# Four pairs of input tiles by seven quarter products over half of the contraction, in a hybrid decoder layer

## The chip, the cores and the metric

The kernel runs on one core of one Trainium2 chip. The metric is device time in microseconds of one execution. The kernel before takes 724.74 us (median of three runs, 724.72 to 724.83).

## What is computed

One layer with two groups of channels side by side, on 1024 tokens and 1024 model channels, in float32. Cut to what matters here:

```python
h = rmsnorm(x, norm_g) * (1.0 + scale[:, None, :]) + shift[:, None, :]
u = h @ w_in                                  # 1024 x 5120
cv, cg, cs, lx, ls = jnp.split(u, [D_CONV, 2 * D_CONV, 3 * D_CONV, 3 * D_CONV + D_LRU], axis=-1)

v = cv * jax.nn.sigmoid(cg)
v = causal_depthwise_conv(v, dw_w, dw_b)      # 31 taps
v = jax.nn.silu(layernorm(v, cln_g, cln_b))
y_conv = (v @ pw2_w + pw2_b) * jax.nn.silu(cs)

xs = causal_depthwise_conv(lx, sc_w, sc_b)    # 4 taps
r = jax.nn.sigmoid(blockdiag(xs, wr) + br)
i = jax.nn.sigmoid(blockdiag(xs, wi) + bi)
a = jnp.exp(-LRU_C * r * softplus(-lam))
hs = linear_scan(a, sqrt(1 - a**2) * (i * xs))
y_lru = hs * jax.nn.silu(ls)

x = x + (1.0 + gate[:, None, :]) * (concat([y_conv, y_lru]) @ w_out)
out = rmsnorm(x, final_g)
```

## The kernel before, in words

**Tiles.** Channels lie on the 128 partitions, tokens along the free dimension. A tile is 128 channels x 1024 tokens; w_in gives 40 of them, numbered by kind: i0 to i7 are the convolution's values (CV), i8 to i15 its GLU gates (CG), i16 to i23 its SiLU gates (CS), i24 to i31 the recurrence's inputs (LX), i32 to i39 its SiLU gates (LS). A contraction over 1024 channels is eight k tiles.

**Three terms.** Each float32 operand is split into a high part in fp32r and the remainder (h and l in the names: uh and ul, whi and wlo). A product is wh x h, wh x l and wl x h, each as one matmul of 128 x 128 by 512 tokens. A plain input tile is 8 k tiles x 3 terms x 2 halves of tokens = 48 matmuls (`mm_k`). The high part is a cast on ACT. The remainder is a subtraction on DVE or GpSimd (POOL in the profile), or ACT writes minus the high part and a transfer on GpSimd's queue adds the original to it (`remainder`, "DMA" in the tables).

**Stages.** First four input tiles while x is normalised (to 56 us); then the slots of the table ORDER, where i is an input tile and g the two gate products of a head of the recurrence; then the recurrence's half of the output projection, its eight output tiles in four pairs (from 471 us), during which the convolution's mean and layer norm are made; then the pointwise projection pw2 and the other half of the output projection; then the last norm.

**Seven products.** The pairs of the second, third and fourth stage already use the seven products of two by two blocks in Winograd's form: two output tiles and two halves of the tokens give a block of four, and the four quarters cost seven products, with sums of weights (S1 to S4) and of tokens (T1 to T4). In the recurrence's pairs (`lru_pair`) this covers half of the contraction, k tiles 0 to 3 (JS); k tiles 4 to 7 are plain halves. Line 1447 is the matmul of these quarters, line 579 that of plain k tiles.

**The convolution.** Its 31 taps run as 16 products of even taps, 16 of sums of neighbouring taps and 15 of odd ones, each over half of the tokens. For most tiles they are multiply-adds on DVE into PSUM (cacc and caccs, line 443); for the tiles in POOLED, ACT makes each product (cq, co) and a transfer on GpSimd's queue adds it into SBUF (es, oo, line 456). csum is the sum of all conv tiles for the mean.

**The order.** A planner (`Plan.order`) lists all operations with a priority, a cost and their dependences, runs a list schedule over PE, ACT, DVE, GpSimd and SP, and emits the instructions in that order; on the chip each engine takes its own in order and waits on semaphores. A slot's priority is its number n; its weights have n - 2.5 (load) and n - 1.4 (split), its evacuation n + 0.5. PSUM holds three tiles of 1024 (mm) and two of 512 (acc), SBUF 47 buffers of one tile (big). `reserve` keeps buffers free of an operation, `S.hold` and `after` make it wait.

**After a gate.** sigmoid, exp, tanh and sqrt on ACT (each change of table is a load), products and a scan on DVE, and the product with the SiLU gate gives y (in sls). yh and yl are its parts, yhs and yls those of the token sums of y0 to y3, held until slot YSLOT.

## Time and profile before

| what | value |
|---|---|
| median of the runs | 724.74 us |
| the profiled execution's span | 723.3 us |
| PE busy | 715.6 us, 3268 matmuls |
| DVE busy | 619.9 us |
| ACT busy | 480.9 us, 44 table loads |
| GpSimd busy | 166.5 us, 169 instructions |
| moved by DMA | 138.06 MB |
| granted TensorE clock, mean | 0.998 |

The span runs from the first to the last instruction; the median is 1.4 us longer than it. A group of instructions is given by line, engine, operation, names of output and inputs without buffer numbers, shapes, count, then busy time and mean ns of one. The time of a matmul in such a group is from its issue to its modelled end and overlaps with the next; the pace is read from the chain in order of time. PEld is the weight load beside the matmul.

### The profile page before, as it was taken

The page shows a single profiled execution, that of the slowest core. Times are in us where ns is not written, and L with a number is a line of the kernel's source. Part 1 is how long each engine was busy: PE and PEld are TensorE (multiplying, and loading weights), DVE is VectorE, ACT ScalarE, POOL GpSimd, SP SyncE. Part 2 cuts the span into 40 slices and gives each one's busy share as a digit, 9 for nine tenths or more (in the row PEclk, how much of TensorE's full clock was granted, in tenths as well). Part 3 has the DMA queues.
Part 4 walks back from the last instruction along what each step waited for, and adds up shares of the span by engine and source line. Part 5 has one row for each costly group of instructions (what it writes and reads, how often), then busy time and mean ns, then how long its engine had stood idle before and what let it go on. Part 6 is the DMA issues. An engine that isn't in the chain of part 4 may idle for free.

```text
span 723.3 us, 9066 instructions
## 1 busy us (share of the span) xinstructions
PE 715.6 (99%) x3268; PEld 596.7 (83%) x3268; DVE 619.9 (86%) x852; ACT 480.9 (66%) x621; POOL 166.5 (23%) x169
## 2 busy tenths in 40 slices
PE   9999999999999999999999999999999999999996
PEld 8888888888888888888888888888888888888886
DVE  7999999989789898789489994998798966999647
ACT  7650689664788956965967879846697635745332
POOL 0036333444534230133221220001101001100001
PEclk9999999999999999999999999999999999999999
DMA  8946439958999997699898896957846755775006
GB/s 334 407 158 191 69 96 239 285 103 197 203 235 211 247 235 154 198 218 233 174 210 225 238 191 144 255 215 169 210 93 145 198 150 140 231 186 181 30 1 232
DMA packets 46635, 138.06 MB, mean 191 GB/s; under 512 B 5264, under 2 KB 16528, under 8 KB 46480
## 3 DMA queue, kind: packets, MB, share of 16 engines
q0 software_dynamic: 19872, 52.88, 41.0%
q1 hardware_dynamic: 25712, 83.71, 32.7%
q10 hardware_dynamic: 1008, 0.92, 0.4%
q8 instruction: 25, 0.41, 0.2%
q14 instruction: 18, 0.15, 0.1%
HBM read 79.11 MB, written 22.54 MB: 141 GB/s over the span
## 4 chain that ended last, share of the span: by engine, by line
PE 98%; DVE 1%; ACT 0%; DVEq 0%; issue 0%
PE ps L579 54%; PE xout L755 6%; PE xpw L755 6%; PE first L888 5%; PE lx L1447 3%; PE ypw L755 3%; PE gate L1308 3%; PE zout L755 2%; PE zpw L755 2%; PE lx L579 2%; PE y L725 1%; PE lc L579 1%; PE yout L755 1%; PE lw L579 1%; PE ld L579 1%; PE late L888 1%
## 5 line engine op out<-in xcount | busy, mean ns | idle before, releaser
L579 PE MATMUL ps<-uh,wlo 128*128 128x512 f32 x576 | 177.4, 389 | 0.0
L579 PE MATMUL ps<-uh,whi 128*128 128x512 f32 x576 | 177.4, 389 | 0.0
L579 PE MATMUL ps<-ul,whi 128*128 128x512 f32 x576 | 177.3, 389 | 0.0
L579 PEld LDWEIGHTS ps<-uh,wlo 128*128 128x128 f32 x576 | 108.1, 188 | 22.5
L579 PEld LDWEIGHTS ps<-ul,whi 128*128 128x128 f32 x576 | 108.1, 188 | 22.4
L579 PEld LDWEIGHTS ps<-uh,whi 128*128 128x128 f32 x576 | 108.0, 188 | 22.4
L424 ACT CAST whi<-raw 128x1024 fp32r<-128x1024 f32 (+1 forms) x44 | 44.9, 1026 | 46.8 <-issue 27.3
L456 POOL DMA_DIRECT2D es<-cq x45 | 40.1, 898 | 135.4 <-ACT cq L432 85.9
L451 POOL TENSOR_TENSOR wlo<-raw,whi 128x1024 fp32r<-128x1024 f32 x16 | 41.0, 2569 | 87.5 <-ACT whi L424 87.1
L432 ACT ACT_TABLE_LOAD x44 | 56.5, 1283 | 1.5 <-PEq L1875 0.7
L443 DVE SCALAR_TENSOR_TENSOR cacc<-v,V,cacc 128x511 f32<-128x511 f32 (+14 forms) x75 | 55.5, 740 | 0.4
L443 DVE SCALAR_TENSOR_TENSOR caccs<-v,V,caccs 128x511 f32<-128x511 f32 (+6 forms) x70 | 52.0, 743 | 1.9 <-ACT caccs L432 1.0
L443 DVE SCALAR_TENSOR_TENSOR caccs<-c,wsum,caccs 128x511 f32<-128x511 f32 (+6 forms) x70 | 52.0, 743 | 1.0
L456 POOL DMA_DIRECT2D oo<-co x39 | 37.5, 995 | 44.8 <-ACT co L432 18.0
L451 DVE TENSOR_TENSOR wlo<-raw,whi 128x1024 fp32r<-128x1024 f32 (+1 forms) x24 | 28.7, 1195 | 8.3 <-ACT whi L424 8.3
L432 ACT ACTIVATE cq<-v,V 128x511 f32<-128x511 f32 (+14 forms) x45 | 31.8, 708 | 4.5 <-DVE modw L443 4.5
L443 DVE SCALAR_TENSOR_TENSOR xs<-ps,V,xs 128x1023 f32<-128x1023 f32 (+2 forms) x24 | 30.6, 1273 | 0.5 <-ACT xs L432 0.5
L432 ACT ACTIVATE cq<-c,wsum 128x512 f32<-128x512 f32 x42 | 29.7, 713 | 0.0
L443 DVE SCALAR_TENSOR_TENSOR modw<-modw,sc 128x1024 f32<-128x1024 f32 x23 | 29.5, 1286 | 0.0
L432 ACT ACTIVATE finsq<-fin 128x512 f32<-128x512 f32 (+2 forms) x14 | 7.9, 570 | 28.5 <-DVE fin L443 15.3
L432 ACT ACTIVATE co<-v,V 128x510 f32<-128x510 f32 (+12 forms) x39 | 26.7, 707 | 0.0
L424 ACT CAST xsh<-xs 128x1024 fp32r<-128x1024 f32 x8 | 8.4, 1050 | 21.8 <-issue 15.9
(447 smaller groups left out, 1592.0 us busy)
## 6 DMA issues: line engine op xcount, KB each, us to landing
raw<-in_w_in_dram SPq DMA_DIRECT2D x36, 512.0 KB, 5.5
modw<-in_mod_w_dram SPq DMA_DIRECT2D x24, 512.0 KB, 8.1
scsd<-scs SPq DMA_DIRECT2D x8, 512.0 KB, 3.9
raw<-in_w_out_dram SPq DMA_DIRECT2D x8, 512.0 KB, 3.6
accd<-acc POOLq DMA_DIRECT2D x8, 512.0 KB, 5.8
rawpw<-in_pw_dram SPq DMA_DIRECT2D x8, 512.0 KB, 4.8
scsr<-scsd SPq DMA_DIRECT2D x8, 512.0 KB, 4.7
rawout<-in_w_out_dram SPq DMA_DIRECT2D x8, 512.0 KB, 3.7
```

The lines of the kernel that those rows point to most:

```text
L424: act.copy(out(), in_())
L432: act.activation(out=out(), in_=in_(), func=func, **kw)
L443: dve.scalar_tensor_tensor(out=out(), in0=in0(), scalar=scalar, in1=in1(), op0=op0, op1=op1, accum_out=accum)
L451: lambda: e.tensor_tensor(out=out(), in0=a(), in1=b(), op=op), prio, r, w,
L456: return S.op("POOL", ISSUE, lambda: pool.dma_start(out(), a(), accum_op=ALU.add), prio, r, w, lag=RATE * n / T, after=after, flight=flight)
L579: pe.matmul(ps()[:, a - off:b - off], k3(lhs)()[:, at, :], rhs[k]()[:, a:b], start=(k == first and lhs is wh and rhs is xh and (a - off) % ...
L725: pe.matmul(to(), half(*lhs)()[:, j * P:j * P + P], half(*rhs)()[:, c0:c1], start=a == "S1" and j == 0 and t == 0, stop=j == KT // 2 - 1 a ...
L755: pe.matmul(half(ps, 0)(), half(*lhs)()[:, j * P:j * P + P], half(*rhs)(), start=start and at == 0 and i == 0, stop=at == len(order) - 1 a ...
L888: pe.matmul(ps()[:, a - off:b - off], fw_part(lhs, k, i * P, i * P + P)(), rhs()[:, a:b], start=k == 0 and lhs is wh and rhs is xh, stop=k ...
L1308: pe.matmul(ps()[:, c0:c1], lhs()[:, j, :], rhs()[:, c0:c1], start=st == 0, stop=st == 2)
L1447: pe.matmul(half(ps, h)(), lhs()[:, o:o + P], half(*rhs)(), start=begin and at == 0 and t == 0, stop=at == len(order) - 1 and t == len(ter ...
```

## The change

**Pairs of input tiles.** The table ORDER gets four entries with a plus: i36+i28, i30+i37, i29+i38 and i22+i18. Such a pair (`duo`) takes two slots. Over k tiles 0 to 3 the four quarters (two tiles, two halves of tokens) come from seven products; over k tiles 4 to 7 each half is a plain sum. w_in is stored with its k tiles in the order 0, 2, 1, 3, 4 to 7, so that a block of weights is contiguous. Four combinations of weights (wz, 256 columns each) are made on GpSimd and split into wsh and wsl; of the second tile only six k tiles are split. The products share two PSUM tiles, up and dn: A11 goes into dn and is copied to up (ACT), S1 into the other half of dn and is copied to wk, and two sums on DVE carry them on.

**Token sums.** From slot 15 on (`token_sums`), GpSimd adds high and low part of h's k tiles 0 to 3, makes the combinations, and splits them (hhs, hls), for all four pairs.

**The convolution.** POOLED goes from tiles 1, 3 and 5 to 1 and 3; tile 5's products become multiply-adds on DVE.

**Beside these.** The order of the other tiles changes, and g5 and g6 change places; four conv tiles instead of three are written out and read back (SPILL); y0 to y3 are written out and read back before their split (YSP); y3, y6 and y7 have their remainder by transfer (YDMA); which engine makes which weight's remainder changes (EARLY, EARLYD, DENG, LRV), and some reserves.

**The order on PE, first pair.** PE, behind A11 and S1 of the first pair (dn27 and up27 are its PSUM tiles, whi27 the first tile's weights, wsh27 and wsl27 the combined ones, uh1 and ul1 k tile 1 of h, hhs01 a token sum, ps29 the plain tile behind the pair):

```order
L599 MATMUL ps29_2781<-uh0_189,whi29_2758 128x512 x2
L599 MATMUL ps29_2781<-ul0_206,whi29_2758 128x512 x2
L599 MATMUL ps29_2781<-uh0_189,wlo29_2767 128x512 x2
L1678 MATMUL up27_2788<-uh1_230,whi27_2678 128x512
L1678 MATMUL up27_2788<-ul1_243,whi27_2678 128x512
L1678 MATMUL up27_2788<-uh1_230,wlo27_2697 128x512
L1678 MATMUL dn27_2754<-hhs01_1813,wsh27_2733 128x512
L1678 MATMUL dn27_2754<-hls01_1850,wsh27_2733 128x512
L1678 MATMUL dn27_2754<-hhs01_1813,wsl27_2746 128x512
L1678 MATMUL dn27_2754<-hhs11_2184,wsh27_2733 128x512
L1678 MATMUL dn27_2754<-hls11_2205,wsh27_2733 128x512
L1678 MATMUL dn27_2754<-hhs11_2184,wsl27_2746 128x512
```

Six matmuls of the next tile stand between S1 and A12, the reader of the copy, and S2 comes in the middle of A12. Before, these slots were 48 matmuls each into one ps.

**The order on PE, where the recurrence's pairs begin.** Before (lx0 and lp0 are PSUM tiles of the first pair, yh7 and yl7 the parts of y7, whi40 weights):

```order
L1447 MATMUL lx0_3855<-yhs11_3891,lsh0_3694 128x512
L1447 MATMUL lx0_3855<-yhs11_3891,lsl0_3745 128x512
L1447 MATMUL lx0_3855<-yls01_3861,lsh0_3694 128x512
L579 MATMUL lp0_3863<-yh7_3837,whi40_3764 128x512 x2
L579 MATMUL lp0_3863<-yl7_3919,whi40_3764 128x512 x2
L579 MATMUL lp0_3863<-yh7_3837,wlo40_3780 128x512 x2
```

and now:

```order
L599 MATMUL lp0_3887<-yh6_3487,whi40_3748 128x512 x2
L599 MATMUL lp0_3887<-yl6_3720,whi40_3748 128x512 x2
L599 MATMUL lp0_3887<-yh6_3487,wlo40_3763 128x512 x2
L1478 MATMUL lx0_3924<-yh0_3774,whi40_3748 128x512
L1478 MATMUL lx0_3924<-yl0_3784,whi40_3748 128x512
L1478 MATMUL lx0_3924<-yh0_3774,wlo40_3763 128x512
L1478 MATMUL lx0_3924<-yh2_3848,whi40_3748 128x512
L1478 MATMUL lx0_3924<-yl2_3870,whi40_3748 128x512
L1478 MATMUL lx0_3924<-yh2_3848,wlo40_3763 128x512
L599 MATMUL lp0_3887<-yh7_3827,whi40_3748 128x512 x2
L599 MATMUL lp0_3887<-yl7_3862,whi40_3748 128x512 x2
L599 MATMUL lp0_3887<-yh7_3827,wlo40_3763 128x512 x2
```

The plain k tiles of y4 to y6 now come first, then A11 (lx0 with y0 and y2), then y7. From the last gate product to the first yh7 there were 167 matmuls and are 126.

**The order on GpSimd's queue.** Before, in the slots ahead of the recurrence's pairs (es5, oo5: conv tile 5; csum: the sum of conv tiles):

```order
L456 DMA es5_2216<-cq5_12_3474 128x1012
L456 DMA csum_2570<-c1_942 128x1024
L456 DMA oo5_2249<-co5_12_3509 128x500
L456 DMA es5_2216<-cq5_13_3532 128x1011
L456 DMA csum_2570<-c6_2645 128x1024
L456 DMA oo5_2249<-co5_12_3509 128x499
L456 DMA es5_2216<-cq5_14_3616 128x1010
L456 DMA oo5_2249<-co5_14_3676 128x498
L456 DMA es5_2216<-cq5_15_3735 128x1009
L456 DMA wlo40_3780<-in_w_out_dram 128x1024
```

and now, ahead of the first pair of input tiles (raw27 and raw28 are its weights):

```order
L466 TENSOR_TENSOR wz27_2657<-raw27_2495,raw28_2614 128x256
L466 TENSOR_TENSOR wz27_2657<-raw28_2614 128x256
L471 DMA csum_2633<-c0_1009 128x1024
L466 TENSOR_TENSOR wz27_2657<-wz27_2657,raw27_2495 128x256
L466 TENSOR_TENSOR wlo27_2697<-raw27_2495,whi27_2678 128x1024
L466 TENSOR_TENSOR wz27_2657<-raw27_2495,wz27_2657 128x256
L471 DMA wlo28_2684<-in_w_in_dram 128x768
L471 DMA es1_1050<-cq1_15_2641 128x1009
L466 TENSOR_TENSOR wsl27_2746<-wz27_2657,wsh27_2733 128x1024
```

The additions of conv tile 5 are gone, and the combinations, one remainder and the split of the combined weights stand between the additions of conv tiles 1 and 3.

The diff, cut to its core:

```diff
@@ -32,21 +32,21 @@
-ORDER = "i24 g0 i10 i2 i11 i3 i26 i25 i33 i12 i4 g1 i34 i18 g2 i13 i5 i27 i35 i19 g3 i14 i6 i20 i28 i36 g4 i15 i7 i29 i37 g5 i30 i38 g6 i31 i39 g7 i23 i21 i22"
+ORDER = "i10 i24 g0 i2 i25 i11 i3 i26 i33 i12 i4 g1 i34 i23 g2 i13 i35 i5 i27 i21 g3 i14 i19 i6 i36+i28 i15 i30+i37 i7 i29+i38 g4 g6 g5 i31 i39 i22+i18 g7 i20"
-SPARE = 5
+SPARE = 3
-HRES = 2
-POOLED = (1, 3, 5)
+HRES = 0
+POOLED = (1, 3)
-SPILL = (0, 2, 4)
+SPILL = (0, 2, 4, 6)
-YHEADS, YSLOT = 2, 36
+YHEADS, YSLOT = 2, 37
+TSETS = 15
+DUOA = 2
+YSP = (0, 1, 2, 3)
+YRES = 5
+TSUB = "POOL"
+WSUB = ("POOL", "POOL", "POOL")
+DENG = {14: ("DMA", "DVE", "DVE"), 15: ("POOL", "DMA", "DVE"), 16: ("DMA", "DVE", "POOL"), 17: ("DMA", "DVE", "DMA"), 18: ("POOL", "POOL", "DMA"), 19: ("DVE", "DVE", "POOL"), 20: ("POOL", "DVE", "POOL"), 21: ("DMA", "DMA", "POOL"), 22: ("DVE", "DVE", "DVE"), 23: ("POOL", "DVE", "POOL"), 24: ("POOL", "DVE", "DMA"), 25: ("POOL", "POOL", "DMA"), 26: ("POOL", "POOL", "POOL"), 27: ("POOL", "DMA", "POOL"), 28: ("POOL", "POOL", "DVE"), 29: ("DMA", "DVE", "DVE"), 30: ("DVE", "DVE", "DVE"), 32: ("POOL", "POOL", "POOL"), 34: ("DMA", "DVE", "DVE"), 35: ("DVE", "DVE", "DMA"), 36: ("POOL", "DMA", "DMA"), 37: ("POOL", "DVE", "DVE"), 38: ("DVE", "DVE", "DVE"), 39: ("DMA", "DVE", "DMA"), 40: ("DMA", "DMA", "DVE"), 41: ("DMA", "DMA", "POOL")}
+YDMA = (3, 6, 7)
+CSUB = "POOL"
-EARLY = 20
-EARLYD = ()
+EARLY = 18
+EARLYD = (14, 28, 30, 31, 32, 33, 38, 40)
-LRV = (1, 2, 4, 5)
+LRV = (0, 2, 4)
...
+        if "+" in x:
+            slots.append(("duo", tuple(int(m[1:]) for m in x.split("+"))))
+        else:
+            slots.append(("gate" if x[0] == "g" else "in", int(x[1:])))
+    wslots = [t for s in slots if s[0] != "gate"
+              for t in ([("in", m) for m in s[1]] if s[0] == "duo" else [s])]
+    wslots += [("lru", m) for m in range(KT)]
...
-        at = LK.index(k) if s[0] == "lru" else k
+        at = LK.index(k)
...
+        if i in YSP:
+            yd = dram.tile([P, T], F32, tag=f"yd{i}", name=f"yd{i}")
+            DMA(pr, lambda: yd, t, FULL_BYTES, r=[t], w=[("yd", i)])
+            t = big_buf(f"yr{i}", parts=2)
+            waiting.append(DMA(B0 - 3 + YSTEP * YORD.index(i), t, lambda: yd, FULL_BYTES, r=[("yd", i)], w=[t], reserve=YRES))
+        p = B0 - 2 + YSTEP * YORD.index(i)
+        if i in YDMA:
+            o = ACT(p, yh[i], t, "copy", r=[t], w=[yh[i]], reserve=SPARE + 1)
+            remainder(p, yl[i], yh[i], t, T, [(yh[i], 0), (yh[i], 1)], [(yl[i], 0), (yl[i], 1)], [t], reserve=SPARE)
+        else:
+            o = split(p, yh[i], yl[i], t, reserve=SPARE)
+        if i < YHEADS and i not in YSP:
...
+    hsets = {}
+    def token_sums(pr, after):
+        for j in JS:
+            a, b = 2 * j, 2 * j + 1
+            x = [big_buf(f"hx{j}{z}", parts=2) for z in (0, 1)]
+            for z, k in enumerate((a, b)):
+                TT(pr, TSUB, x[z], lambda k=k: hh[k]().bitcast(F32), lambda k=k: hl[k]().bitcast(F32), ALU.add,
+                   r=[hh[k], hl[k]], w=[x[z]], after=after, reserve=TRES)
+            x0, x1 = x
+            def sub(to, a, b):
+                TT(pr, TSUB, half(*to), half(*a), half(*b), ALU.subtract, H, r=[a, b], w=[to])
+            sub((x0, 0), (x0, 1), (x0, 0))
+            sub((x0, 1), (x1, 1), (x0, 1))
+            sub((x1, 1), (x1, 1), (x0, 0))
+            sub((x1, 0), (x1, 0), (x1, 1))
+            sets = []
+            for z, t in enumerate(x):
+                hi, lo = (big_buf(f"h{h}s{j}{z}", F32R, 2) for h in "hl")
+                split(pr, hi, lo, t, eng=TSUB)
+                sets.append((hi, lo))
+            (c, d), (e, f) = sets
+            for q, hi, lo, z in (("B11", hh[a], hl[a], 0), ("B21", hh[b], hl[b], 0), ("B22", hh[b], hl[b], 1),
+                                 ("T1", c, d, 0), ("T3", c, d, 1), ("T4", e, f, 0), ("T2", e, f, 1)):
+                hsets.setdefault(q, []).append((hi, lo, z))
+    def duo(m0, m1, n):
+        rest = LK[2 * NJ:]
+        s0, s1 = ("in", m0), ("in", m1)
+        q, w_ = n - 1.4, NJ * P
+        for s, where in ((s0, None), (s1, DUOW)):
+            w_bufs(s, where)
+            DMA(n - 2.5, k3(raw[s]), lambda s=s: wsrc(s)[:, :, :], FULL_BYTES, w=[raw[s]])
+        r0, r1 = raw[s0], raw[s1]
+        def kk(b, i):
+            return [(b, k) for k in range(i * NJ, i * NJ + NJ)]
+        z, sh, sl = big_buf(f"wz{n}", parts=4), big_buf(f"wsh{n}", F32R), big_buf(f"wsl{n}", F32R)
+        def block(b, i):
+            return part(b, i * w_, i * w_ + w_)
+        for to, (a, ai, ak), (b, bi, bk) , op in (
+                (0, (r0, 0, kk(r0, 0)), (r1, 0, kk(r1, 0)), ALU.subtract),
+                (3, (r1, 0, kk(r1, 0)), (r1, 1, kk(r1, 1)), ALU.add),
+                (2, (z, 3, [(z, 3)]), (r0, 0, kk(r0, 0)), ALU.subtract),
+                (1, (r0, 1, kk(r0, 1)), (z, 2, [(z, 2)]), ALU.subtract)):
+            TT(q, CSUB, block(z, to), block(a, ai), block(b, bi), op, w_, r=ak + bk, w=[(z, to)],
+               after=[started[n - DUOA]])
+        for s, k in ((s0, 0), (s1, NJ)):
+            hi, lo, r = whi[s], wlo[s], raw[s]
+            cut = lambda b, k=k: (lambda: k3(b)()[:, k:, :])
+            keys = lambda b, k=k: [(b, i) for i in range(k, KT)]
+            ACT(q, cut(hi), cut(r), "copy", (KT - k) * P, r=keys(r), w=keys(hi), after=[started[n - DUOA]])
+            w_eng = DENG.get(n, WSUB)[k > 0]
+            if w_eng == "DMA":
+                remainder(q, cut(lo), cut(hi), lambda s=s, k=k: wsrc(s)[:, k:, :], (KT - k) * P, keys(hi), keys(lo))
+            else:
+                SUB(q, w_eng, cut(lo), cut(r), cut(hi), (KT - k) * P, r=keys(r) + keys(hi), w=keys(lo))
+        z_eng = DENG.get(n, WSUB)[2]
+        if z_eng == "DMA":
+            ACT(q + KQ, sh, z, "copy", r=[z], w=[sh])
+            remainder(q + KQ, sl, sh, z, T, [sh], [sl], [z])
+        else:
+            split(q + KQ, sh, sl, z, eng=z_eng)
+        wq = {"S3": (sh, sl, 0, 0), "S4": (sh, sl, 1, 0), "S2": (sh, sl, 2, 0), "S1": (sh, sl, 3, 0),
+              "A11": (whi[s0], wlo[s0], 0, None), "A12": (whi[s0], wlo[s0], 1, None),
+              "A22": (whi[s1], wlo[s1], 1, None)}
+        up, dn = mm_tile(f"up{n}"), mm_tile(f"dn{n}")
+        ops = {}
+        def quarter(g, a, b, ps, h, begin):
+            wh, wl, i, key = wq[a]
+            rk = [(wh, key), (wl, key)] if key is not None else kk(wh, i) + kk(wl, i)
+            for j, (bh, bl, z) in enumerate(hsets[b]):
+                def emit(j=j, bh=bh, bl=bl, z=z):
+                    o = (i * NJ + j) * P
+                    for t, (lhs, rhs) in enumerate(((wh, bh), (wh, bl), (wl, bh))):
+                        pe.matmul(half(ps, h)(), lhs()[:, o:o + P], half(rhs, z)(),
+                                  start=begin and j == 0 and t == 0, stop=j == NJ - 1 and t == 2,
+                                  skip_group_check=True)
+                o = S.op("PE", 3 * (H + 32) / 2400, emit, n + g, rk + halves(bh, z * H, z * H + H) + halves(bl, z * H, z * H + H),
+                         [(ps, h)], columns=3 * H)
+                ops.setdefault(a, o)
+        def plain(g, s, ps, h):
+            for k in rest:
+                mm_k(n + g, ps, s, hh, hl, k, FULL[h:h + 1], first=-1)
+        quarter(0.0, "A11", "B11", dn, 0, True)
+        ACT(n + FORKN, half(up, 0), half(dn, 0), "copy", H, r=[(dn, 0)], w=[(up, 0)])
+        quarter(0.1, "S1", "T1", dn, 1, True)
+        kept = big_buf(f"wk{n}")
+        ACT(n + FORKN, half(kept, 0), half(dn, 1), "copy", H, r=[(dn, 1)], w=[kept])
+        quarter(0.2, "S2", "T2", dn, 0, False)
+        TT(n + FORKN, "DVE", half(up, 1), half(dn, 0), half(kept, 0), ALU.add, H, r=[(dn, 0), kept], w=[(up, 1)])
+        quarter(0.3, "A12", "B21", up, 0, False)
+        plain(0.3, s0, up, 0)
+        quarter(0.4, "S3", "T3", dn, 0, False)
+        TT(n + FORKN, "DVE", half(dn, 1), half(dn, 0), half(kept, 0), ALU.add, H, r=[(dn, 0), kept], w=[(dn, 1)])
+        quarter(0.5, "S4", "B22", up, 1, False)
+        plain(0.5, s0, up, 1)
+        quarter(0.6, "A22", "T4", dn, 0, False)
+        plain(0.6, s1, dn, 0)
+        plain(0.7, s1, dn, 1)
+        return ops["A11"], ops["S3"], up, dn
...
+        if s[0] == "duo":
+            for m in s[1]:
+                hooks(n)
+                n += 1
+            n -= 2
+            started[n], started[n + 1], *tiles = duo(*s[1], n)
+            s_n = n
+            for m, ps in zip(s[1], tiles):
+                after_start(n)
+                evac_in(m, ps, s_n + DUOE * (m == s[1][1]), ev=EVD)
+                if m // KT * KT == CV:
+                    conv_tile(m % KT)
+                n += 1
+            n -= 1
+            continue
...
-        "w_in": w_in,
+        "w_in": w_in[:, :, LK],
```

63 lines of the change are left out of this document (36 added, 27 removed).

## The prediction

> **What bounds the kernel now.** I read the engine totals first, then the chain that ended last in order of time, then all waits of PE, then windows of the stages in which the four pairs lie.
>
> ```profile
> span 723.3 us, 9066 instructions
> PE 715.6 (99%) x3268; PEld 596.7 (83%) x3268; DVE 619.9 (86%) x852; ACT 480.9 (66%) x621; POOL 166.5 (23%) x169
> PE 98%; DVE 1%; ACT 0%; DVEq 0%; issue 0%
> ```
> ```profile
> 120.09 81.60 PE ps L579 x360
> ...
> 441.06 29.92 PE ps L579 x132
> ...
> 478.91 1.36 PE lp L579 x6
> ...
> 500.57 1.36 PE lx L1447 x6
> 501.94 1.36 PE ld L1447 x6
> ```
> ```profile
> PE token_stats L845 <- DVE ones L501: 1.1, 1, 1.1
> PE finbc L802 <- ACT finsqz L432: 0.3, 1, 0.3
> PE finbc L808 <- DVE rs65.7_0_5837 L819: 0.2, 1, 0.2
> ```
>
> TensorE is the whole chain: each piece begins where the last one ended, and its waits for other engines are 1.6 us in the whole span, none between the first projections and the last norm. 360 matmuls of 512 columns in 81.60 us are 0.2267 us each. The quarter products that the second projection already has (line 1447, lx and ld) run at the same pace, 1.36 / 6. So a matmul taken out of the middle is worth 0.2267 us, if everything PE reads still arrives in time. The question is whether DVE, at 86%, and the transfers can keep up with a PE that asks earlier.
>
> **What is removed from PE.** A pair of input tiles is 2 x 8 x 3 x 2 = 96 matmuls. The new pair is 7 quarter products of 2 x 3, which is 42, and four halves over the other four k tiles, 4 x 4 x 3 = 48: 90. Four pairs save 24 matmuls, 24 x 0.2267 = **5.44 us**. The profiled execution would go from 723.3 to 717.9 us; what lies around the span (724.74 - 723.3 = 1.4 us) stays, so the median would be 719.3 us with nothing lost.
>
> **The forks inside a pair.** A11 is copied from dn to up, S1 to wk (ACT), and two sums are made on DVE. The second projection has the same pattern:
>
> ```profile
> L424 ACT COPY lc<-lx 128x512 f32<-128x512 f32 x3 | 1.8, 585 | 0.0
> L451 DVE TENSOR_TENSOR ld<-lx,lk 128x512 f32<-128x512 f32 x3 | 2.1, 692 | 0.0
> L432 ACT ACT_TABLE_LOAD x44 | 56.5, 1283 | 1.5 <-PEq L1875 0.7
> ```
>
> The order of PE puts 12 matmuls (S1 and six of another tile, 2.72 us) between A11 and the first reader of its copy, and 21 (4.76 us) between S2 and S3, which waits for the first sum. A copy of 0.59 us even behind a table load and an activation of about 1 us (2.9 us together) would be late by 0.2 us, in four pairs 0.8 us; the lower end is nothing. I take 0, since PE ran this pattern without a gap at 500 us.
>
> **What DVE, ACT and GpSimd get.** Conv tile 5 goes from products on ACT, added by GpSimd's transfers, to DVE: 44 more multiply-adds. Beside these: 8 sums of 512 (0.69), 2 more remainders wsl, 5 fewer wlo and 3 fewer yl on DVE.
>
> ```profile
> core 0: us, PE busy (x) PEld busy (x) DVE busy (x) ACT busy (x) POOL busy (x), PEclk, DMA share, GB/s
> 202.00:495.60 293.60, 293.60 (x1296) 242.88 (x1295) 252.71 (x294) 223.31 (x269) 70.20 (x78) 1.00 0.89 212
> ```
> ```profile
> L443 DVE SCALAR_TENSOR_TENSOR cacc<-v,V,cacc 128x511 f32<-128x511 f32 (+14 forms) x75 | 55.5, 740 | 0.4
> L451 DVE TENSOR_TENSOR yl<-sls,yh 128x1024 fp32r<-128x1024 f32 x8 | 9.6, 1219 | 1.1 <-ACT yh L424 1.1
> L432 ACT ACTIVATE cq<-v,V 128x511 f32<-128x511 f32 (+14 forms) x45 | 31.8, 708 | 4.5 <-DVE modw L443 4.5
> L456 POOL DMA_DIRECT2D es<-cq x45 | 40.1, 898 | 135.4 <-ACT cq L432 85.9 <-issue 23.6 <-DMA es<-cq 12.4
> L451 POOL TENSOR_TENSOR wlo<-raw,whi 128x1024 fp32r<-128x1024 f32 x16 | 41.0, 2569 | 87.5 <-ACT whi L424 87.1 <-PE late L888 0.3
> L451 POOL TENSOR_TENSOR o<-fin,bc 128x256 f32<-128x256 f32 x5 | 3.6, 742 | 10.5 <-ACT bc L424 10.5
> ```
>
> DVE: 44 x 0.74 + 8 x 0.69 - 6 x 1.22 = 32.6 + 5.5 - 7.3 = 30.8 us, nearly all in the stage from 202 us to the mean of the convolution (495.6). It had 293.6 - 252.7 = 40.9 us free there, and the window gets 5.4 us shorter: 4.7 us stay free. Two such multiply-adds in a row start 0.65 us apart (129.30 and 129.95, below), which gives 44 x 0.09 = 4.0 us back: 4.7 to 8.7 us. That is 97 to 98% of the stage, hidden only while nothing else holds DVE.
>
> ACT loses 44 products net (31 us at 0.71) and gets eight casts (token sums, combined weights), eight copies and seven scalings ahead of transfers (about 20 us at 0.59 to 1.05): it stays under 223 us of 288. GpSimd loses 29 issues (26 us), gets 7 (6 us), ten tensor operations of 1024 (25.7), eight of 512 (10.4, twice the half), sixteen of 256 (16 x 0.74 = 11.9) and one of 768 (1.9): 49.9 us of tensor work. 70 becomes about 100 us of 288: room enough, but these operations and DVE's meet:
>
> ```profile
> 129.30 0.73 DVE L443 SCALAR_TENSOR_TENSOR caccs<-c,wsum,caccs 128x501 f32<-128x501 f32 x1
> 129.95 0.73 DVE L443 SCALAR_TENSOR_TENSOR cacc<-v,V,cacc 128x500 f32<-128x500 f32 x1
> ...
> 137.65 3.01 DVE L451 TENSOR_TENSOR sls<-sls,r 128x1024 f32<-128x1024 f32 x1
> ...
> 149.14 3.90 DVE L443 SCALAR_TENSOR_TENSOR caccs<-v,V,caccs 128x511 f32<-128x511 f32 x5
> ```
> ```profile
> 137.18 2.39 POOL L451 TENSOR_TENSOR wlo<-raw,whi 128x1024 fp32r<-128x1024 f32 x1 [4.06 <-ACT whi L424]
> ...
> 148.06 2.41 POOL L451 TENSOR_TENSOR wlo<-raw,whi 128x1024 fp32r<-128x1024 f32 x1 [5.27 <-ACT whi L424]
> ```
> ```profile
> L1320 DVE TENSOR_TENSOR_SCAN r<-a,xs 128x1024 f32<-128x1024 f32 x8 | 20.5, 2565 | 0.1
> L451 DVE TENSOR_TENSOR sls<-sls,r 128x1024 f32<-128x1024 f32 x8 | 11.5, 1442 | 0.1
> L451 DVE TENSOR_TENSOR xsl<-xs,xsh 128x1024 fp32r<-128x1024 f32 x8 | 11.1, 1386 | 0.2 <-ACT xsh L424 0.2
> 454.30 2.29 DVE L1320 TENSOR_TENSOR_SCAN r<-a,xs 128x1024 f32<-128x1024 f32 x1
> ```
>
> The product with both inputs in SBUF took 3.01 us while GpSimd worked, against 1.22 for one of its kind (yl): 1.79 lost. The multiply-adds whose sum is in PSUM took 3.90 for five beside the other operation, so at most 0.6 more than five starts of 0.65. Over the span scan, sls and xsl lost 8 x (2.565 - 2.29 + 1.442 - 1.22 + 1.386 - 1.22) = 5.3 us to sixteen GpSimd operations, 0.33 us each. The new work is 49.9 / 2.57 = 19.4 such operations: 6.4 us lost. Bounds are 0 and 19.4 x 1.79 = 34.7; I take 6.4, since most of DVE's time in this stage goes to sums in PSUM. 6.4 against 4.7 to 8.7 free: just hidden, 0 in the sum.
>
> The Trainium skill (SBUF — State Buffer, section "Who interferes with whom") says that a DVE instruction with two SBUF inputs and a GpSimd instruction that reads SBUF exclude each other for a whole instruction. The 3.01 us agree, and so does the run in PSUM. By that rule alone nothing limits the loss to the 6.4 us, which is the last rival below.
>
> **The join at y7**, where the pairs of the second projection begin. Gate 7 now comes later and its remainder yl7 is a transfer instead of a DVE instruction (so are yl6 and yl3).
>
> ```profile
> 440.44 0.62 PE L1308 MATMUL gate<-xsh,glo 128*128 128x512 f32 x2
> 453.91 0.62 ACT L424 COPY c<-caccs 128x512 f32<-128x512 f32 x1
> 462.50 2.93 ACT L424 CAST yh<-sls 128x1024 fp32r<-128x1024 f32 x3
> DMA to landing us min/median/max: 4.6/7.2/9.8
> ```
>
> From the end of the gates to the first use of yh7 there were 478.91 - 441.06 = 37.9 us. In the new order there are 126 matmuls, 28.6 us, and 0.4 more until yl7: 29.0. What has to happen: dn37 ends 54 matmuls on (12.2); ACT evacuates it (0.95, the pace of the casts, 2.93 / 3), makes two copies into c7 (1.1) and yh1 (0.95); DVE makes yl1 and a half of c7 (1.8); ACT scales (0.65), then yh7, yhs00, yh2, yh3 and the start of yl7 (5 x 0.95 = 4.75): 22.4. The transfer lands 7.2 us after its issue (the row is that of ylc, the same form and size), 29.6: **0.6 us late**. Landings of 4.6 or 9.8 make it 0 or 3.2. I take 0.6.
>
> The Trainium skill (DMA: Bandwidth & Descriptors, section "Anatomy of one DMA — SWDGE (gpsimd) path") gives about 2.0 us and the bytes at 436 GB/s for such a transfer, an estimate of 3.2 us for 512 KB. No accumulating transfer of this trace is so fast; by the page the term would be 0 and the time 719.3.
>
> Behind the waiting matmul stands the whole second projection on PE, and behind yh7 on ACT the casts of the four y that were read back, so nothing makes up for a late yl7: what it is late is added to the end.
>
> **Queues.** SP gets ten more transfers of 512 KB (four y written out and read back, one c), while GpSimd's queue loses 29 accumulations (11 MB) and gains 7.
>
> ```profile
> raw<-in_w_in_dram SPq DMA_DIRECT2D x36, 512.0 KB, 5.5
> cr<-cd SPq DMA_DIRECT2D x3, 512.0 KB, 4.4
> ```
>
> A y that is written out waits on SP for its last product on DVE, and the next weights queue behind it. These loads land in 5.5 us and stand two to three tiles (22 to 33 us) ahead of their use, so a wait of DVE's length (3 us) is covered: 0. If it were not, one late weight tile would cost what it is late. The reloads start with slot 37, whose first matmul stands 48 matmuls (10.9 us) ahead of the last one of gate 7, and yh0 is cast behind the evacuation of up37, 24 matmuls later: 16 us against 4.4. The token sums start at slot 15, twelve tiles before their first reader: 0.
>
> Sum: 724.74 - 5.44 + 0.6 = **719.9 us**.
>
> **Rivals.**
>
> *A, the forecast*, 0.62: PE stays fed, 719.9 (719.1 with nothing lost, 721.2 with 0.8 at the forks and half of the slow landing). For it: no wait of PE in the stage before.
>
> *B, slow landings at the join*, 0.14: 3.2 us lost, 724.74 - 5.44 + 3.2 = 722.5. For it: three accumulations and wlo41 follow each other on GpSimd's queue. Against it: accumulations in pairs are usual in this trace.
>
> *C, DVE becomes the bound*, 0.12: the loss to GpSimd is double (12.8), 4.1 over the 8.7 free, and the mean waits: 723.4. Against it: part of the 40.9 us was waiting that a fuller queue only fills.
>
> *D, slower*, 0.09: the same place, but DVE's two-input operations meet GpSimd's new ones as sls did, in half of the cases: 17.4 lost, 8.7 over, 724.74 - 5.44 + 8.7 = 728.0. It decides from 8.7 + 5.4 + 1.5 = 15.6 us lost, 0.80 per operation. Against it: 0.33 measured.
>
> *E, no gain*, 0.03: another limit gives the 5.4 us back, 724.7.
>
> Measurements of this kernel tell 0.2% (1.45 us) from no change. Faster: A, B but 0.01, a third of C, 0.79. Same: 0.01 of B, 0.07 of C, E, 0.11. Slower: D and the rest of C, 0.10. The range 718.9 to 723.3 holds A, B and nearly half of C, 0.81.
>
> **What would show it.** PE: 3244 matmuls, about 710 us busy, pace 0.2267. Right: no PE wait above 0.3 us before 460 us, one of at most 1.5 us at lp<-yl. B: the wait there exceeds 2 us, released by the transfer. C and D: DVE at 97% or more in 202 to 490, sls, scan and wlo longer than 1.8 us, and PE waiting for csl, xsl or the sums of a pair. I am wrong if PE waits inside the pairs for wsh or wsl, GpSimd's chain, which in the first pair is four operations of 256, two of 1024 and three issues (3.0 + 5.1 + 2.7 = 10.8 us) and has two tiles (96 matmuls, 21.8 us) for it.

## The result: 728.66 us, slower by 0.55%

The changed kernel took 728.66 us (median of four runs, 728.47 to 729.29) against 724.79 for the kernel before on the same chip (724.72 to 725.02), a ratio of 1.0055, 95% interval 1.0041 to 1.0070. The forecast was 719.9 with a range to 723.3. The profiled span grew from 723.3 to 726.0 us.

From the page of the profile after: span, engine totals, and the shares of the chain that ended last.

```profile
span 726.0 us, 9074 instructions
PE 713.5 (98%) x3244; PEld 593.0 (82%) x3244; DVE 655.7 (90%) x898; ACT 474.7 (65%) x601; POOL 206.1 (28%) x181
PE 76%; DVE 16%; issue 3%; ACT 3%; DMA 1%; DVEq 0%; POOL 0%; ACTq 0%; POOLq 0%
```

The 24 matmuls are gone (3268 to 3244). But PE, which was 98% of the chain, is now 76%, and DVE is 16% of it. PE's waits of the kernel after, the longest first (us in total, times, longest):

```profile
PE ps L599 <- ACT r L447: 3.6, 1, 3.6
PE token_stats L865 <- DVE ones L516: 1.1, 1, 1.1
PE ly L599 <- DMA wlo<-in_w_out_dram: 0.7, 1, 0.7
```

One new wait stands out. It lies at 204 us, far ahead of the pairs. The windows of the kernel after around it, and over the stage that the prediction averaged:

```profile
core 0: us, PE busy (x) PEld busy (x) DVE busy (x) ACT busy (x) POOL busy (x), PEclk, DMA share, GB/s
187.00:204.00 17.00, 17.00 (x77) 14.08 (x76) 16.72 (x14) 7.30 (x9) 17.00 (x13) 1.00 0.70 172
204.00:208.00 4.00, 0.56 (x3) 0.13 (x1) 3.93 (x6) 2.93 (x4) 2.52 (x2) 1.00 1.01 185
208.00:212.00 4.00, 3.88 (x10) 3.07 (x11) 3.15 (x4) 1.56 (x4) 2.28 (x3) 0.57 0.56 100
...
202.00:495.60 293.60, 289.10 (x1264) 237.68 (x1263) 279.35 (x336) 212.09 (x242) 100.13 (x84) 0.99 0.75 192
```

The kernel before in the first of these windows:

```profile
187.00:204.00 17.00, 17.00 (x76) 14.08 (x75) 11.07 (x15) 10.30 (x14) 7.00 (x7) 1.00 0.99 207
```

From 187 to 204 us GpSimd is now busy without a pause (7.00 us before) and DVE does 14 instructions in 16.72 us (15 in 11.07 before). Then PE stands, and when it comes back the granted clock is 0.57 for 4 us: ten matmuls where about 18 would fit.

**The chain of the stall.** DVE in the kernel after, by time (start, us, operation):

```profile
187.59 5.24 DVE L458 SCALAR_TENSOR_TENSOR modw<-modw,sc 128x1024 f32<-128x1024 f32 x1
...
193.36 7.03 DVE L458 SCALAR_TENSOR_TENSOR caccs<-v,V,caccs 128x511 f32<-128x511 f32 x9
200.29 4.69 DVE L458 SCALAR_TENSOR_TENSOR modw<-modw,sc 128x1024 f32<-128x1024 f32 x1
```

The same two products in the kernel before:

```profile
187.34 1.22 DVE L443 SCALAR_TENSOR_TENSOR modw<-modw,sc 128x1024 f32<-128x1024 f32 x1
...
202.87 1.22 DVE L443 SCALAR_TENSOR_TENSOR modw<-modw,sc 128x1024 f32<-128x1024 f32 x1
```

GpSimd after, in the same stretch:

```profile
185.40 2.73 POOL L466 TENSOR_TENSOR wlo<-raw,whi 128x1024 fp32r<-128x1024 f32 x1
187.76 2.73 POOL L466 TENSOR_TENSOR hx<-uh,ul 128x1024 f32<-128x1024 f32 x1
190.13 1.60 POOL L466 TENSOR_TENSOR hx<-hx 128x512 f32<-128x512 f32 x1
191.38 1.19 POOL L471 DMA_DIRECT2D es<-cq  x1
...
200.55 3.34 POOL L466 TENSOR_TENSOR hls<-hx,hhs 128x1024 fp32r<-128x1024 f32 x1
```

ACT, where the wait ends:

```profile
205.07 1.05 ACT L439 CAST hhs<-hx 128x1024 fp32r<-128x1024 f32 x1 [9.99 <-DVE modw L458]
206.02 1.04 ACT L439 CAST whi<-raw 128x1024 fp32r<-128x1024 f32 x1
206.97 1.11 ACT L447 ACTIVATE r<-gate,V 128x1024 f32<-128x1024 f32 x1
```

PE, the matmuls on both sides:

```profile
203.94 0.61 PE L1329 MATMUL gate<-xsh,glo 128*128 128x512 f32 x2
208.12 1.17 PE L599 MATMUL ps<-uh,whi 128*128 128x512 f32 x2 [3.57 <-ACT r L447]
```

`modw` multiplies a tile of modulation weights by sc; both of its inputs and its output lie in SBUF. Before, it took 1.22 us both times. Now the token sums (hx, hls) occupy GpSimd, and the first is held over two of them, the second until hls ends: 5.24 + 4.69 - 2 x 1.22 = 7.5 us. The nine multiply-adds between them, whose sum is in PSUM, run on at 0.78 each. The second `modw` matters to ACT: the token sum's cast hhs writes into the buffer that this `modw` reads, so it waits 9.99 us. Two places behind it in ACT's queue stands the sigmoid r of head 1, which reads the PSUM tile that PE's next slot (ps) wants. So a cast that nobody needs for a hundred microseconds stops PE.

From start to start of matmuls, what goes beyond 0.2267 us sums to 1.36 us before and 9.02 after. Of the 7.66 more, 5.45 are this place (a gap of 3.96, then eight matmuls at 0.43), 1.0 the first use of wlo of the second projection at 484 us, 1.2 small delays of at most 0.4 each. -5.44 + 7.66 = 2.2 us, and PE's last matmuls start at 718.98 instead of 716.60, 2.4 later. Another 0.4 us lies behind them: together the 2.7 us by which the profiled span grew. What lies around the span, taken run by run, is 2.43 us against 1.88 in runs of the kernel before, 0.55 more. That is 3.3 us; between the medians it is 3.9.

The groups of DVE that the hold can touch, after and then before:

```profile
L458 DVE SCALAR_TENSOR_TENSOR modw<-modw,sc 128x1024 f32<-128x1024 f32 x23 | 37.0, 1611 | 0.0
L466 DVE TENSOR_TENSOR wlo<-raw,whi 128x1024 fp32r<-128x1024 f32 (+1 forms) x19 | 23.9, 1259 | 1.2 <-ACT whi L439 1.1
L1341 DVE TENSOR_TENSOR_SCAN r<-a,xs 128x1024 f32<-128x1024 f32 x8 | 19.8, 2480 | 0.0
L466 DVE TENSOR_TENSOR sls<-sls,r 128x1024 f32<-128x1024 f32 x8 | 11.8, 1475 | 0.1
L466 DVE TENSOR_TENSOR xsl<-xs,xsh 128x1024 fp32r<-128x1024 f32 x8 | 10.3, 1286 | 0.0
```
```profile
L443 DVE SCALAR_TENSOR_TENSOR modw<-modw,sc 128x1024 f32<-128x1024 f32 x23 | 29.5, 1286 | 0.0
```

modw alone went from 29.5 to 37.0 us, while scan, sls and xsl together lost a little less than before.

### The profile page after: what moved, and what is told of

Read it like the earlier page. It is cut to its first block, busy times and chain, and to the rows that moved or that the text cites. A ratio compares the mean times of both kernels' runs of the same rounds, so it can differ in the third digit from the quotient of the medians.

```text
span 726.0 us, 9074 instructions
## 1 busy us (share of the span) xinstructions
PE 713.5 (98%) x3244; PEld 593.0 (82%) x3244; DVE 655.7 (90%) x898; ACT 474.7 (65%) x601; POOL 206.1 (28%) x181
## 4 chain that ended last, share of the span: by engine, by line
PE 76%; DVE 16%; issue 3%; ACT 3%; DMA 1%; DVEq 0%; POOL 0%; ACTq 0%; POOLq 0%
PE ps L599 25%; PE xout L775 6%; PE xpw L775 6%; PE first L908 5%; DVE caccs L458 5%; PE dn L1678 3%; PE up L599 3%; PE ypw L775 3%; PE lx L1478 3%; DVE xs L458 2%; PE dn L599 2%; DVE cacc L458 2%; PE gate L1329 2%; PE zout L775 1%; PE zpw L775 1%
## 5 line engine op out<-in xcount | busy, mean ns | idle before, releaser
L599 PE MATMUL ps<-uh,whi 128*128 128x512 f32 x448 | 139.1, 392 | 3.6 <-ACT r L447 3.6
L599 PE MATMUL ps<-uh,wlo 128*128 128x512 f32 x448 | 138.4, 390 | 0.0
L599 PE MATMUL ps<-ul,whi 128*128 128x512 f32 x448 | 138.3, 390 | 0.0
L599 PEld LDWEIGHTS ps<-uh,whi 128*128 128x128 f32 x448 | 84.3, 189 | 21.7 <-ACT r L447 4.0
L599 PEld LDWEIGHTS ps<-ul,whi 128*128 128x128 f32 x448 | 84.5, 189 | 17.7
L599 PEld LDWEIGHTS ps<-uh,wlo 128*128 128x128 f32 x448 | 84.4, 188 | 17.6
L466 POOL TENSOR_TENSOR wlo<-raw,whi 128x1024 fp32r<-128x1024 f32 (+1 forms) x17 | 44.5, 2628 | 81.4 <-ACT whi L439 81.0
L458 DVE SCALAR_TENSOR_TENSOR cacc<-v,V,cacc 128x511 f32<-128x511 f32 (+14 forms) x90 | 66.8, 743 | 0.8 <-ACT cacc L447 0.5
L471 POOL DMA_DIRECT2D oo<-co x26 | 25.5, 982 | 34.6 <-ACT co L447 12.3
L471 POOL DMA_DIRECT2D lz<-in_w_out_dram x16 | 14.2, 960 | 26.2 <-ACT lz L447 24.2
```

The costliest lines, as they stand in the source:

```text
L458: dve.scalar_tensor_tensor(out=out(), in0=in0(), scalar=scalar, in1=in1(), op0=op0, op1=op1, accum_out=accum)
L466: lambda: e.tensor_tensor(out=out(), in0=a(), in1=b(), op=op), prio, r, w,
L471: return S.op("POOL", ISSUE, lambda: pool.dma_start(out(), a(), accum_op=ALU.add), prio, r, w, lag=RATE * n / T, after=after, flight=flight)
L599: pe.matmul(ps()[:, a - off:b - off], k3(lhs)()[:, at, :], rhs[k]()[:, a:b], start=(k == first and lhs is wh and rhs is xh and (a - off) % ...
```

## The experiments

The theory to start from: GpSimd's token sums hold DVE, the held `modw` blocks ACT's queue, and PE waits behind it. The first rival: DVE is full with the 44 multiply-adds more, and a repaired stall comes back a little later. In the diffs, a MOVES entry takes one operation, found by its engine and the names of its tiles, and puts it behind another of the same engine; everything else keeps its order and its tiles in SBUF. The kernel before, run again beside each of the four groups of runs: 725.14, 724.71, 724.75 and 724.59 us; each ratio is to the runs of its own group.

### One cast moved behind the sigmoid

```diff
+MOVES = [("ACT", ("hx01", "hhs01"), ("ACT", ("gate1_0", "r1")))]
```

> The changed kernel with one instruction moved: ACT's cast of the token sum hhs01 stands behind the sigmoid r1 (of gate1_0), not two instructions ahead of it. Everything else in its order and place. Theory (lock, then queue): GpSimd's token sums hold the products of modw16 and modw17 on DVE; hhs01 takes modw17's buffer, so its cast waits, and r1 and with it the PSUM tile of ps17 wait behind the cast. Then modw16 and modw17 still take about 5.2 and 4.7 us, but PE's gap of 3.96 us at ps17 and the eight matmuls at half pace go: 728.66 - 3.73 - 1.7 = 723.2 us. Rival (DVE has too much to do in this part of the program): the stall comes back within the next 30 us of PE, and the time stays at 727 or more.

727.80 us, ratio 1.0034 (1.0021 to 1.0048). The gap at 204 us shrank from 3.96 to 1.52, and two new ones came. PE's waits of this kernel:

```profile
PE ps L618 <- ACT scs L466: 1.9, 1, 1.9
PE gate L1348 <- DVE xsl L485: 1.3, 1, 1.3
PE ps L618 <- ACT r L466: 1.1, 1, 1.1
```

The chain through ACT's queue was real: without it the gap at 204 is 2.4 us smaller. But the rival's figures came true, 727 us or more and a stall within 30 us. For the gap of 2.31 us at 230, DVE and then ACT:

```profile
210.21 1.21 DVE L485 TENSOR_TENSOR v<-ps,sig 128x1024 f32<-128x1024 f32 x1
```
```profile
211.45 1.12 ACT L466 ACTIVATE g<-gate,V 128x1024 f32<-128x1024 f32 x1 [4.49 <-DVE v L485]
...
231.30 1.02 ACT L466 ACTIVATE scs<-ps 128x1024 f32<-128x1024 f32 x1
```

The evacuation v stands on DVE behind the second `modw`, which still takes 4.73 us, and a wlo of 2.58. ACT's g waits for v, and from g to scs, for which PE waits, ACT has no idle time. So this stall is still the lateness that the first batch of token sums left in DVE and ACT. In the changed kernel PE was 5.4 us late itself and ACT waited for it at 231 us. The second batch holds DVE too (a wlo of 5.78 us at 231.87), but PE's gap had begun at 230.06. That DVE has too much work, the rival's reason, isn't shown here.

### The order of the two splits exchanged on GpSimd

```diff
+MOVES = [("POOL", ("hx00", "hhs00", "hls00"), ("POOL", ("hx01", "hhs01", "hls01")))]
```

> The changed kernel with one instruction moved on GpSimd: the split hls00 stands behind the split hls01, so that no tensor operation of GpSimd runs while DVE comes to modw17; ACT's order is as it was. Theory: modw17 takes 1.2 to 1.3 us in place of 4.69, hhs01 is cast some 3.4 us earlier, and PE's gap at ps17 falls from 3.96 to under 1 us with no matmuls at half pace behind it: 723.5 to 724.5 us. Rival (the order of ACT alone, hhs01 waits for something other than modw17): the gap stays, 728.7 us. Rival (DVE has too much to do): 727 or more, with the stall elsewhere.

726.92 us, ratio 1.0034 (1.0021 to 1.0046). The second `modw` now takes 1.22 us, with hls out of its way: the hold is caused by the GpSimd operation beside it. The time that the theory gave (723.5 to 724.5) did not come. PE stood for 1.92 us at 204, 1.27 at 230 and 1.70 at 292. At 204 it now waits for v, which stands on DVE behind the first `modw`, still held (5.18 us):

```profile
205.99 0.73 PE L618 MATMUL ps<-uh,whi 128*128 128x512 f32 x2 [1.53 <-DVE v L485]
```

And r1 writes into the buffer that hls00 reads, and hls00 is later now. From r1 on ACT has no idle time until scs, for which PE waits at 230:

```profile
209.43 1.12 ACT L466 ACTIVATE r<-gate,V 128x1024 f32<-128x1024 f32 x1 [5.94 <-POOL hls L485]
```

### The cast moved, and one late weight by DVE

```diff
-LRV = (0, 2, 4)
+LRV = (0, 1, 2, 4)
```

with the move of the first experiment. The remainder of the second output weight is then made by DVE instead of an accumulating transfer, which had landed 10.7 us after its issue.

> As the first kernel of this call, and the remainder wlo41 (the second tile of the recurrence's first pair) made by DVE, not by a transfer that landed 10.68 us after its issue. Theory: PE's gap of 1.12 us at ly0 goes too, with the slow matmul behind it: 1.0 us less than the first kernel, 722.2 us. Rival (DVE is full around the join): the sums yls or the sums of the convolution come late in its place, 723.2 or more.

727.08 us, ratio 1.0033 (1.0021 to 1.0044). The wait at the start of the second projection is gone, as expected, and those at 204, 229 and 291 us (1.04, 2.30 and 1.69) stay. It did not clearly bring its microsecond. Between the profiles of the first experiment and this one PE's last matmul moves 1.3 us earlier, but 1.1 of that is there already at 292 us, ahead of the weight; behind 478 us small gaps appeared.

### Four GpSimd operations into gaps between DVE's

```diff
+MOVES = [("POOL", ("hx00",), 1, ("POOL", ("es1", "cq1_6"), 0)),
+         ("POOL", ("uh1", "ul1", "hx01"), 0, ("POOL", ("hx00",), 1)),
+         ("POOL", ("hx00", "hhs00", "hls00"), 0, ("POOL", ("es1", "cq1_7"), 0)),
+         ("POOL", ("hx10",), 1, ("POOL", ("es1", "cq1_9"), 0))]
```

with the late weight by DVE as in the experiment above.

> The changed kernel with four operations of GpSimd moved so that its tensor operations no longer stand in a row when DVE comes to modw16, modw17 and the remainder at 231 us: hx01 and the first difference of hx00 behind the addition es1 of product 6, hls00 behind that of product 7, the first difference of hx10 behind that of product 9; and wlo41 made by DVE. Nothing is left out. Theory (GpSimd's runs hold DVE): modw16 and modw17 fall from 5.2 and 4.7 us to under 2.5 each, the stalls of PE at 204, 230 and 292 us that the first two kernels showed shrink from about 5 us together to under 2, and the time is 722.5 to 724.5. Rival (DVE has too much to do, whoever holds it): 726.5 or more, as before this move.

727.10 us, ratio 1.0032 (1.0019 to 1.0044). The first `modw` was held all the same (5.90 us), the second was free (1.22), and the next instruction with two SBUF inputs took its place: wlo at 203.92, 4.61 us. So the hold went to another instruction of DVE. PE stood for 2.60 us at 204, and that wait ends with r1, which waits for the hls that was moved:

```profile
205.16 1.11 ACT L465 ACTIVATE r<-gate,V 128x1024 f32<-128x1024 f32 x1 [1.33 <-POOL hls L484]
```

### Token sums left out, taps left out, both left out

Three kernels take away work and keep the order. In the first, GpSimd's additions and splits of the token sums become plain transfers on its queue, and the differences are eight columns wide; in the second, conv tile 5's 44 multiply-adds are eight columns wide; the third has both.

```diff
-                TT(pr, TSUB, half(*to), half(*a), half(*b), ALU.subtract, H, r=[a, b], w=[to])
+                few = lambda b, z: part(b, z * H, z * H + 8)
+                TT(pr, TSUB, few(*to), few(*a), few(*b), ALU.subtract, H, r=[a, b], w=[to])
...
-                split(pr, hi, lo, t, eng=TSUB)
+                ACT(pr, hi, t, "copy", r=[t], w=[hi])
+                S.op("POOL", p_cost(T), lambda lo=lo: pool.dma_start(lo(), hh[a]()), pr, [t, hi, hh[a]], [lo])
```
```diff
-            STT(pr, cut(acc_e, r, H), cut(ev, 0, H - r), w(2 * r), cut(acc_e, r, H), ALU.mult,
+            e, n = (r + 8 if i == 5 else H), (8 if i == 5 else H - r)
+            STT(pr, cut(acc_e, r, e), cut(ev, 0, n), w(2 * r), cut(acc_e, r, e), ALU.mult,
...
```

> The changed kernel in its order, but GpSimd's token sums are left out: the full additions and the splits are plain transfers of other data on GpSimd's queue, the differences are 8 columns wide. The pairs then multiply wrong data in the same number of instructions. Theory (the sums hold DVE's operations with two inputs in SBUF, some 10 to 14 us between 187 and 245 us): modw16 and modw17 take 1.2 to 2.5 us, PE has no stall over 1 us between 200 and 300 us, 722.5 to 724 us with the wait for wlo41 left. Rival (44 multiply-adds more are too many for DVE): 726.5 or more.

> The changed kernel in its order, but 44 multiply-adds of conv tile 5 on DVE are 8 columns wide (its sums are then wrong); some 25 us of DVE's work from about 268 us on are left out. Theory (the sums are the cause): the stall of 3.96 us at ps17 and the eight matmuls behind it stay, and the time changes by less than 0.7 us: 728.0 to 728.8. Rival (44 multiply-adds more are too many): 725 or less.

> Both left out: GpSimd's token sums and 44 multiply-adds of conv tile 5. The bound of what the 24 matmuls can give in this order. Theory: as with the sums alone left out, 722.5 to 724. Rival (too many multiply-adds): 2 us or more below the kernel with the sums alone left out.

| left out | median us | ratio to before | largest gap of PE |
|---|---|---|---|
| nothing (the changed kernel) | 728.66 | 1.0055 (1.0041 to 1.0070) | 3.96 at 204 us |
| token sums | 730.22 | 1.0071 (1.0056 to 1.0087) | 4.44 at 289 us |
| taps of tile 5 | 728.02 | 1.0042 (1.0027 to 1.0057) | 3.69 at 204 us |
| both | 724.25 | 1.0002 (0.9984 to 1.0020) | 1.22 at 480 us |

Without the sums, the group of `modw` between 180 and 290 us is back at its free duration (16.0 us for seven in the changed kernel), and no wait is left at 204. That part of the theory came true, its time (722.5 to 724) did not: PE now stands for the recurrence's xsl instead:

```profile
L458 DVE SCALAR_TENSOR_TENSOR modw<-modw,sc 128x1024 f32<-128x1024 f32 x7 | 8.5, 1217 | 2.8 <-DMA modw<-in_mod_w_dram 2.8
```
```profile
PE gate L1329 <- DVE xsl L466: 4.0, 1, 4.0
```

Without the taps, the wait at 204 is nearly whole, as the theory said:

```profile
PE ps L599 <- ACT r L447: 3.3, 1, 3.3
```

Without both, xsl is 0.4 late, and between the first projections and 460 us no other wait above 0.2 us is left:

```profile
PE ly L599 <- DMA wlo<-in_w_out_dram: 0.8, 1, 0.8
PE gate L1331 <- DVE xsl L466: 0.4, 1, 0.4
```

So there are two causes. The hold alone gives the stall at 204. The taps alone give one at 289, which in the changed kernel is covered, because PE is 5.4 us late by then. Taking out the taps alone gains 0.6 us, taking out the sums alone costs 1.6, taking out both gains 4.4 (6.0 less than without the sums, as the rival said). One reservation belongs to the sums' kernel: its DVE waits 2.8 us at 264 for a transfer that the changed kernel does not wait for. The kernel without both has the same wait (3.0 us) and is only 0.4 late, so 3.6 of the 4.0 go with the taps, yet not all 3.6 would show without that transfer; the first two experiments, where the stall at 204 is shortened and DVE is not kept waiting, show 1.3.

The last kernel also says what the change has left with both causes out: 724.25, spread over ten runs from 722.92 to 728.73. That is no gain over 724.71 that can be told from noise, although 24 matmuls are gone. In its profile PE's excess is 4.35 us (1.36 before): 1.0 at the late weight, 0.5 at xsl, 1.5 in small gaps, some of them at the forks. With 0.8 us more behind the last matmul and 0.5 around the span, about 4.3 of the 5.44 us are spoken for.

### The tables chosen again

If the hold is what the written order leaves out of account, an order that counts it should do better. The tables were chosen again by a replay in which a DVE instruction with two SBUF inputs waits for a run of GpSimd operations. All parts of the change stay. The three best, the middle one cut to its core:

```diff
-ORDER = "... g3 i14 i19 i6 i36+i28 i15 i30+i37 i7 i29+i38 g4 g6 g5 i31 ..."
+ORDER = "... g3 i14 i21 i19 i6 i36+i28 i15 i30+i37 g4 i7 i29+i38 g6 g5 i31 ..."
-TSETS = 15
+TSETS = 16
-YDMA = (3, 6, 7)
+YDMA = (1, 2)
-LRV = (0, 2, 4)
+LRV = (0, 2, 3, 4, 7)
...
```

> A third set of tables found in the same way, nearer to the order of the changed kernel. Theory: 721 to 724.5. Rival: 725 or more.

> The changed kernel with all its parts (four pairs, token sums on GpSimd, conv tile 5 on DVE); only the tables of the order, of priorities, of reserves and of the engines of remainders are others. They were chosen by counting, for a written order, how long DVE's operations with two inputs in SBUF wait when GpSimd's tensor operations follow each other without a gap, which the kernel's planner does not count. Theory (the time is lost because DVE's queue is written without room for these holds): no stall of PE over 2 us between 180 and 480 us, its excess over 0.227 us per matmul falls from 9.0 us to under 5, and the time is 720.5 to 724. Rival (the work that went to DVE does not fit, in whatever order): 725 or more.

> Another set of tables found in the same way, with the combinations of weights on DVE and fewer remainders on it. Theory: 720.5 to 724. Rival: 725 or more.

737.37 us (1.0175, 1.0160 to 1.0190), 725.22 (1.0007, 0.9998 to 1.0017) and 732.56 (1.0106, 1.0084 to 1.0128). The second is the best full version found: 3.4 us under the changed kernel, and even with the kernel before. None came into the range that was expected, and two fell far behind it, so the replay does not carry the timing of this stretch. PE's waits of the second, and the DVE instruction behind the first of them:

```profile
PE ps L599 <- DVE v L466: 2.7, 1, 2.7
PE gate L1329 <- DVE xsl L466: 1.2, 1, 1.2
```
```profile
199.48 5.62 DVE L458 SCALAR_TENSOR_TENSOR modw<-modw,sc 128x1024 f32<-128x1024 f32 x1
...
205.04 1.21 DVE L466 TENSOR_TENSOR v<-ps,sig 128x1024 f32<-128x1024 f32 x1
```

Again a `modw` at 200 us, now in DVE's own queue ahead of the evacuation v that PE needs.

### Two repairs of the best one

```diff
+MOVES = [("DVE", ("modw18", "sc"), 0, ("DVE", ("ps16", "v4"), 0))]
```

> The first replanned kernel with one instruction moved on DVE: the product of modw18, which GpSimd held for 5.6 us at 199.5 us, stands behind the evacuation v of ps16 (whose input is in PSUM), for which PE waited 2.7 us. Theory (in a full queue a held instruction costs what stands behind it): the gap of 3.13 us at 203 us goes, and the matmuls at half pace behind it, some 4.3 us; but DVE is no earlier at 292 us, so the wait for xsl there grows from 1.2 us by as much as DVE is short of: between 721 and 725 us. Rival (the hold alone counts, its place in the queue does not): 725.2, the gap stays.

726.76 us, 1.0030 (1.0020 to 1.0039), slower than without the move: the gap at 203 us is gone, and PE stands for 1.59 at 229 and 2.38 at 290 (xsl) with seven matmuls at half pace behind. The second repair adds, for that xsl, seven multiply-adds of tile 5 and one wlo behind it:

```diff
+         ("DVE", ("raw25", "wlo25"), 0, ("DVE", ("xs3", "xsl3"), 0)),
+         ("DVE", ("v5", "cacc5"), 0, ("DVE", ("c4", "caccs4"), -1))] + [("DVE", ("v5", "cacc5"), 0, None)] * 6
```

> As the kernel beside it, and seven multiply-adds of conv tile 5 and one remainder (wlo of slot 25), which nobody waits for, stand behind the remainder xsl of head 3, for which the gates wait, not ahead of it. Theory: the stall at 292 us falls by 3 us or more against the kernel beside it, and the time is 720.5 to 723, faster than before. Rival (DVE is short of time altogether, so what is moved back is missed later): no better than the kernel beside it.

728.03 us, 1.0040 (1.0028 to 1.0052). The stall at 290 is gone, and one of 2.71 us is at 321, inside the first pair, soon followed by one of 1.29 and eleven half-pace matmuls:

```profile
PE dn L1697 <- POOL wsl L485: 2.3, 1, 2.3
```

This is the chain that the prediction names last, GpSimd's for wsl in the first pair. It takes about as long as was reckoned there (11.2 us against 10.8), but its first operation waits 5.90 us for DVE's scan. Each repair made the stall smaller or took it away where it was made, and each time PE stood a few tens of microseconds later: from 204 to 229 to 290 to 321 us.

## Why the prediction was wrong

**The saving: right.** 24 matmuls at 0.2267 us are gone, and the pairs themselves are fed: inside them PE waits 0.2 us (for the copy wk), against 0 taken and 0.8 as the bound.

**The loss to GpSimd: the size right, the conclusion wrong.** Here the prediction failed. It priced 6.4 us by 0.33 per operation, set it against 4.7 to 8.7 us free, and took "just hidden, 0 in the sum". By the same groups and free durations, the loss after is 23 x (1.611 - 1.217) for modw, 4.1 for scan, sls and xsl and about 1.6 in others, 14.8 in all, against 6.9 before: 7.9 us more. But 7.5 of it fell on two instructions within 17 us, and in place of 0 PE lost 5.45 us behind them. The 0.33 came from GpSimd operations that stood apart (87.5 us idle before the sixteen); in a row they hold one DVE instruction over several of them.

**The average over 293 us: the wrong measure.** DVE had 14.2 us free in 202 to 495.6 us after the change (8.8 if the window is taken 5.4 us shorter, as forecast), not less than the 4.7 to 8.7 of the forecast, and PE stood all the same. What decides is the slack up to the next instruction that PE needs: r1 at 204 and, in the kernel without sums, xsl at 289. The stage was also taken too late: the averaged window begins at 202 us, and the two holds begin at 187.59 and 200.29.

**"The token sums start at slot 15 … : 0": wrong.** Their reader is far off, which was checked; what stands behind them was not. They brought buffers, casts and GpSimd time into slots 15 to 18, and the cast hhs01, with no slack on its buffer, stood ahead of r1 on ACT.

**The price of a stall: not in the sum.** Behind a gap of 3.96 us, eight matmuls ran at 0.43 us. That is 1.7 us of the loss.

**The join: right in size, wrong in place.** 0.6 was forecast for a late yl7. yl7 came in time; a later accumulating transfer in GpSimd's queue, wlo, was late by 0.7 us. That the size fits is luck. Rows of PE, and the issue:

```profile
484.21 0.39 PE L599 MATMUL ly<-yl,whi 128*128 128x512 f32 x1
485.33 0.50 PE L599 MATMUL ly<-yh,wlo 128*128 128x512 f32 x1 [0.74 <-DMA wlo<-in_w_out_dram]
```
```profile
wlo<-in_w_out_dram POOLq DMA_DIRECT2D x1, 384.0 KB, 10.7
```

The rivals had named this queue, with landings up to 9.8 us.

**What lies around the span "stays": wrong by 0.55 us**, and 0.4 more behind the last matmul. (The 1.4 us of the forecast is a median less the span of one execution; run by run it is 1.88.) Neither is explained: the replanned kernel has 1.84 us around its span, like the kernel before, so it isn't a price of the pairs as such.

**The rivals.** D forecast 728.0, close to 728.66, and its mechanism is the one that the runs show: DVE's operations with two SBUF inputs meet GpSimd's new ones. It had 0.09, because it was to decide only from 15.6 us lost, spread over the stage; 7.9 sufficed. Its place was wrong too (the mean instead of r1 and xsl), and the closeness of its number is luck: the 8.7 us that it lost at the mean are in the profile 5.45 at r1, 1.0 at a late weight, 1.2 in small delays and about 0.9 behind the last matmul and around the span. C was right that DVE becomes a bound, as the kernel without sums shows, at another place. The sign to look for, no PE wait above 0.3 us before 460 us, was the right one: PE waited 3.6 us. The signs set for C and D did not appear as written: DVE was at 95% of 202 to 490 us, not 97, and the hold fell on modw, which they don't name (sls took 1.475 us and wlo 1.259, both below 1.8).

What stays open: whether some order makes the change pay. No part of the saving was seen at the end of any full version, and the half with conv tile 5 back on transfers was only tried by narrowing its multiply-adds, not by a new order for it.
